# Both parts of the values side by side in a hybrid decoder trunk: 512-column products for a pair of heads, upper keys split too, the block branch stacked

## Chip, cores and metric

The kernel runs on one core of a Trainium2 chip. The metric is the device time of one execution in microseconds (us); less is better. Engines are named as in the profile: PE is the matrix engine (PEld its weight loads), DVE the vector engine, ACT the scalar engine, POOL the GpSimd engine, SP the queue that issues the transfers.

## What is computed

The reference is a two-layer decoder trunk on 256 positions of width 2048, all in float32:

```python
for i in range(DEPTH):                       # DEPTH = 2
    h = rms_norm(x, norm_mix[i])
    x = x + (nsa_mixer(h, ...) if i % 2 == 0 else pool_mixer(h, ...))
    h = rms_norm(x, norm_ffn[i])
    x = x + swiglu(h, ffn_w_gu[i], ffn_w_down[i])
return rms_norm(x, norm_final)
```

The change lies in `nsa_mixer` of layer 0. It has 32 query heads in 4 groups that share keys and values; a key has 96 columns, a value 64. Each head has three attention branches: over 15 compressed blocks (the block branch), over selected blocks, and over a sliding window. At 256 positions selection and window both come out as causal attention over all positions, each with its own keys and values. Each branch is a masked softmax of scores plus a bias by distance, times the values; the three results are weighted by sigmoid gates and added, and the result of all heads is multiplied by `w_out`.

## The kernel before

**Numbers in two parts.** A float32 weight is loaded as `wraw`, copied by ACT into a high part `whi` (L134) in the type fp32r, and DVE subtracts that to give the low part `wlo` (L135). Activations are held in two parts in the same way, next to each other: `xg[k]` is 128 x 512, 256 columns of high part and then 256 of low part. A product is high x high, high x low and low x high. `gemm` (L170) does it as three matmuls of 256 columns for each of 16 steps of k (lines 166 to 168) into one 256-column sum. `gemm2` (L190) sends the high weights once over all 512 columns (L186) and the low weights over 256 (L185, L188), so two sums lie side by side in the bank; `whole` (L216) then adds them: ACT copies one half out (L219), DVE adds the other (L220).

**The stages.** First norm, key and value projections and block compression; then the attention loop over the heads; then the output projection `w_o`, and the feed-forward and pooling stages, all of which stream their weights through PE. The weights come in blocks of 128 x 1024 in one fixed order (`stream`); five blocks are loaded ahead and three are split ahead.

**The attention loop** runs over 8 quads of heads. A quad's queries need three products over `xg` (each 16 steps of k), split into parts by L642 (ACT) and L643 (DVE). Then it goes over two pairs of heads:

- `scores` (L521), for each head: nine matmuls into `ps_s` (three buffers), DVE adds scale and bias on the way out (L540) into `prob` (128 x 768: upper and lower half of the positions, two branches) and into `pc` for the block branch; maxima on DVE (L551, L553), exponentials with their sums on ACT (L557), reciprocals and gates on DVE (L559, L560), scaling on ACT (L563) and DVE (L565).
- `block_scores` (L569), for each pair: one maximum on DVE (L574), four exponentials on ACT (L577), a reciprocal (L579), gate, scale and mask on POOL (L580 to L585).
- `turned` (L588), for each head: four PE transposes (L592) of the probabilities of keys 0 to 127 into `ps_t` (two buffers), a high part by ACT (L595) and a low part by DVE (L596), each 128 x 512.
- `turned_rest` (L599), for each pair: four transposes (L603) of the probabilities of keys 128 to 255 (only the upper 128 positions have any), copied by ACT as plain float32 (L605); two transposes of the block probabilities (L608), copied by DVE (L611, 64 x 256).
- `outputs` (L614), for each head: six matmuls of 256 columns (L620 to L622) with the values `v0h`, `v0l` as weights. The values stand with 64 columns of zeros on each side, and the 128-column slice is taken so that an even head lands in the upper and an odd head in the lower half of the partitions of one sum `ps_o` (one buffer, 128 x 256).
- `outputs_rest` (L624): for each pair four matmuls of 128 columns with plain float32 values (L630; each appears as two instructions in the profile) and one of 256 columns for the block branch (L632, also two).
- ACT and DVE then split `ps_o` into `oT` (L654, L655).

**What sets the order.** The order of each engine's instructions is fixed when the program is built: a planner walks the program with its own model of durations and gives each engine, in turn, the earliest-written instruction that is ready by that model. On the chip every engine works through its list in order. So the query products of the next quad, and near the end the first columns of the output projection (`own=j == 0`, L750), are woven between the steps of a pair. The bias of a head is loaded four heads ahead (L514, L535).

Of the kernel before, what the change touches and what calls it, by code (L numbers as in the profile page):

```python
# [17 lines left out]
P = 128  # L18
# [24 lines left out]
VPAD = (2 * G + 1) * DV  # L43
# [19 lines left out]
def nsa_pool_trunk(ctx, tc, xT, xn, gain0, small, band, gfin, w_kc, w_qk, w_vg, w1k, w1v, w_o,  # L63
# [217 lines left out]
    v0 = {a: ap.tile([P, 2, VPAD], F32R, name=f"v0{a}") for a in "hl"}  # L281
    v1 = ap.tile([P, 2, VPAD], F32, name="v1")
    vc = ap.tile([2 * CB, G, P], F32, name="vc")
# [3 lines left out]
    pcs = [ap.tile([P, 2, 2, CB], F32, name=f"pc{i}") for i in range(3)]  # L287

    def values(t):

        return t[:, DV:].rearrange("p (g z d) -> p g z d", g=G, z=2)[:, :, 0, :]
# [3 lines left out]
    with tc.tile_pool(name="first", bufs=1, reuse_waits="tile") as fp, \  # L295
# [45 lines left out]
        for t in (v0["h"], v0["l"], v1, vc):  # L341
            nc.gpsimd.memset(t.bitcast(F32) if t.dtype == F32R else t, 0.0)
        for t in pcs:
            nc.gpsimd.memset(t, 0.0)
# [107 lines left out]
        def block_values():  # L452
            hv = yield from hidden(vab, "b1v", "v")
            pv = bank()[:NC, :G * DV]
            w2 = col("w2v").rearrange("p (h d) -> p h d", h=2)
            for g in range(G):
                for h in range(2):
                    nc.tensor.matmul(pv[:, g * DV:(g + 1) * DV], hv[:, h, g * CS:g * CS + NC],
                                     w2[:, h], start=h == 0, stop=h == 1)
            for i in range(2):  # L460
                nc.scalar.activation(vc[i * CB:i * CB + NC, :, i * DV:(i + 1) * DV],
                                     pv.rearrange("n (g d) -> n g d", g=G), AF.Copy)


        def row_values(br):
# [15 lines left out]
            h0, l0 = (values(v0[a][:, br]) for a in "hl")  # L481
            nc.scalar.activation(h0, src[0], AF.Copy, scale=rcol[:, 0:1])
            for g in range(G):
                nc.vector.scalar_tensor_tensor(l0[:, g], src[0][:, g], rcol[:, 0:1],
                                               h0[:, g].bitcast(F32), op0=OP.mult, op1=OP.subtract)
            nc.scalar.activation(values(v1[:, br]), src[1], AF.Copy, scale=rcol[:, 1:2])
# [25 lines left out]
    def load_bias(h):  # L512

        bias[h] = hp.tile([P, 400], F32, name="bias", bufs=4)  # L514
        nc.sync.dma_start(bias[h], bass.AP(tensor=skew.tensor, offset=skew.offset + h * 528,
                                           ap=[[1, P], [1, 400]]))
# [4 lines left out]
    def scores(h, qs, pc):  # L521
# [12 lines left out]
        if h + 4 < NH:  # L534
            load_bias(h + 4)  # L535
# [9 lines left out]
        logits(pc[:, 1, e, :CS], ps[0][:, :CS], 1, CB - 1, [[-CS, CS]])  # L545
        logits(view(p, P, [[S, 2], [1, P]]), ps[1], 1, P, two)
        logits(p[:, 512:], ps[2][:, CS:], 0, P, two)
        logits(pc[:, 0, e, :CS], ps[2][:, :CS], 0, P + CB - 1, [[-CS, CS]])
# [20 lines left out]
    def block_scores(h, pc):  # L569

        x = pc[:, :, :, :CS]
        mx = hp.tile([P, 2, 2], F32, name="mxc")
        su = hp.tile([P, 2, 2], F32, name="suc")
        nc.vector.tensor_reduce(mx, x, axis=AX.X, op=OP.max, negate=True)  # L574
        for t in range(2):
            for e in range(2):
                nc.scalar.activation(x[:, t, e], x[:, t, e], AF.Exp, bias=mx[:, t, e:e + 1],  # L577
                                     accum_out=su[:, t, e:e + 1])
# [3 lines left out]
        for t in range(2):  # L582
            nc.gpsimd.tensor_tensor(x[:, t], x[:, t], su[:, t, :, None].to_broadcast([P, 2, CS]),
                                    op=OP.mult)
            nc.gpsimd.tensor_tensor(x[:, t], x[:, t], m[:, t, None, :].to_broadcast([P, 2, CS]),  # L585
                                    op=OP.mult)

    def turned(p):  # L588

        ps = psA.tile([P, 512], F32, name="ps_t", bufs=2)  # L590
        for i, o in enumerate((512, 0, 640, S)):
            nc.tensor.transpose(ps[:, i * P:(i + 1) * P], p[:, o:o + P], ident)  # L592
        th = hp.tile([P, 512], F32R, name="th", bufs=3)
        tl = hp.tile([P, 512], F32R, name="tl", bufs=3)
        nc.scalar.activation(th, ps, AF.Copy)  # L595
        nc.vector.tensor_tensor(tl, ps, th.bitcast(F32), op=OP.subtract)  # L596
        return th, tl

    def turned_rest(p2, pc):  # L599

        ps = psA.tile([P, 512], F32, name="ps_t", bufs=2)
        for i, (p, o) in enumerate(((p2[0], P), (p2[0], S + P), (p2[1], P), (p2[1], S + P))):
            nc.tensor.transpose(ps[:, i * P:(i + 1) * P], p[:, o:o + P], ident)  # L603
        t1 = hp.tile([P, 512], F32, name="t1", bufs=2)
        nc.scalar.activation(t1, ps, AF.Copy)  # L605
        ps = psA.tile([P, 512], F32, name="ps_t", bufs=2)
        for t in range(2):
            nc.tensor.transpose(ps[:2 * CB, t * P:(t + 1) * P],  # L608
                                pc[:, t].rearrange("p e n -> p (e n)"), ident)
        tcm = hp.tile([2 * CB, S], F32, name="tcm", bufs=2)  # L610
        nc.vector.tensor_copy(tcm, ps[:2 * CB, :S])  # L611
        return t1, tcm

    def outputs(h, po, th, tl):  # L614
        g, odd = h // HG, h % 2
        c = DV * (2 * g + 1 - odd)
        for br in range(2):
            va, vb = (v0[a][:, br, c:c + P] for a in "hl")
            xa, xb = th[:, br * S:(br + 1) * S], tl[:, br * S:(br + 1) * S]
            nc.tensor.matmul(po, va, xa, start=not odd and br == 0, stop=False)  # L620
            nc.tensor.matmul(po, va, xb, start=False, stop=False)
            nc.tensor.matmul(po, vb, xa, start=False, stop=False)  # L622

    def outputs_rest(h, po, t1, tcm):  # L624
        g = h // HG
        for e in range(2):
            c = DV * (2 * g + 1 - e)
            for br in range(2):
                i = 2 * e + br
                nc.tensor.matmul(po[:, P:], v1[:, br, c:c + P], t1[:, i * P:(i + 1) * P],  # L630
                                 start=False, stop=False)
        nc.tensor.matmul(po, vc[:, g, :], tcm, start=False, stop=True)  # L632

    for h in range(4):
        load_bias(h)
    for q in range(NH // 4):
# [3 lines left out]
        for j in range(3):  # L640
            ps = whole(gemm2(xg), "up")
# [3 lines left out]
        for h in range(4 * q, 4 * q + 4, 2):  # L645
            pc = pcs[h // 2 % 3]
            p2 = [scores(i, q4 if i % 4 == 3 else q3[:DK, i % 4], pc) for i in (h, h + 1)]
            block_scores(h, pc)
            po = psA.tile([P, 512], F32, name="ps_o")[:, :S]
            for e in range(2):  # L650
                outputs(h + e, po, *turned(p2[e]))
            outputs_rest(h, po, *turned_rest(p2, pc))
            o = oT[h // 2]
            nc.scalar.activation(o[:, :S], po, AF.Copy)  # L654
            nc.vector.tensor_tensor(o[:, S:], po, o[:, :S].bitcast(F32), op=OP.subtract)  # L655
# [293 lines left out]
```

## Time and profile before

| | us |
|---|---|
| median of 3 runs | 2148.22 |
| lowest and highest | 2146.88, 2149.23 |
| the profiled execution | 2149.3 |
| its span, first to last instruction | 2146.6 |
| PE busy / weight loads busy | 2122.3 / 1788.1 |
| DVE busy / ACT busy / POOL busy | 1190.1 / 1055.4 / 62.7 |

In a group's line the numbers behind the bar are the busy time of the whole group in us and the mean duration of one in ns; in a timeline a line begins with the start and the duration in us. A matmul's duration is much longer than the distance to the next one, because they are pipelined: what a matmul costs PE is the distance from its start to the next start. The same holds, by less, for DVE and ACT.

### The profile page before, as it was taken

The numbers are of one execution on the slowest core, as the hardware profiler recorded it, in microseconds if no ns is written. First come the engines' busy times: TensorE is split into PE (matmuls) and PEld (weight loads), VectorE is DVE, ScalarE is ACT, GpSimd is POOL, SyncE is SP. The second block draws the span as 40 slices with busy tenths as digits, with TensorE's granted clock in tenths as the row PEclk, the third lists the DMA queues.
The fourth block names the chain that finished last, engine by engine and source line by source line (L and its number), as shares of the span: only waits on it lengthen the run. The fifth ranks groups of instructions, "written<-read, shape, count | busy, mean of one in ns | idle before, by whom it ended". The sixth has DMA issues, their size and how long they took to land.

```text
span 2146.6 us, 27425 instructions
## 1 busy us (share of the span) xinstructions
PE 2122.3 (99%) x10412; PEld 1788.1 (83%) x10412; DVE 1190.1 (55%) x1534; ACT 1055.4 (49%) x1602; POOL 62.7 (3%) x138
## 2 busy tenths in 40 slices
PE   8999999999999999999999999999999999999997
PEld 7899888888888888888888888888888888888886
DVE  7768888555455445554444555555444554444443
ACT  5578787454444444444344454544444444434443
POOL 4000011000000000000000000000000000000000
PEclk9999999999999999999999999999999999999999
DMA  6674444666666666666666656666666666676664
GB/s 234 193 225 137 143 138 119 193 182 192 189 190 187 192 188 194 188 187 195 188 192 190 196 174 185 184 189 186 190 190 190 192 184 191 189 212 192 193 194 127
DMA packets 115267, 396.78 MB, mean 185 GB/s; under 512 B 13088, under 2 KB 19488, under 8 KB 114880
## 3 DMA queue, kind: packets, MB, share of 16 engines
q1 hardware_dynamic: 115088, 394.97, 61.1%
q8 instruction: 81, 1.33, 0.3%
q14 instruction: 50, 0.41, 0.1%
q10 hardware_dynamic: 48, 0.07, 0.0%
HBM read 391.25 MB, written 2.16 MB: 183 GB/s over the span
## 4 chain that ended last, share of the span: by engine, by line
PE 98%; POOL 1%; DVE 0%; ACT 0%; DMA 0%; issue 0%; SPq 0%; DVEq 0%; POOLq 0%; ACTq 0%
PE acc L212 26%; PE acc L211 26%; PE acc L213 26%; PE acc L186 5%; PE acc L185 2%; PE turn L737 1%; PE ps_t L592 1%; PE acc L166 1%; PE ps_o L630 1%; PE acc L168 1%; PE acc L167 1%; POOL kab L388 1%; PE ps_s L529 1%; PE ps_s L531 1%; PE ps_s L530 1%; PE turn L703 0%
## 5 line engine op out<-in xcount | busy, mean ns | idle before, releaser
L135 DVE TENSOR_TENSOR wlo<-wraw,whi 128x1024 fp32r<-128x1024 f32 (+1 forms) x727 | 886.8, 1221 | 847.0 <-ACT whi L134 840.8
L134 ACT ACTIVATE whi<-wraw 128x1024 fp32r<-128x1024 f32 (+1 forms) x727 | 765.6, 1053 | 912.4 <-PE acc L213 851.3
L213 PE MATMUL acc<-whi,xg 128*128 128x512 f32 x1536 | 599.8, 390 | 0.0
L212 PE MATMUL acc<-wlo,xg 128*128 128x512 f32 x1536 | 598.3, 390 | 0.0
L211 PE MATMUL acc<-whi,xg 128*128 128x512 f32 x1536 | 545.8, 390 | 0.0
L212 PEld LDWEIGHTS acc<-wlo,xg 128*128 128x128 f32 x1536 | 288.4, 188 | 59.3
L213 PEld LDWEIGHTS acc<-whi,xg 128*128 128x128 f32 x1536 | 288.3, 188 | 59.3
L211 PEld LDWEIGHTS acc<-whi,xg 128*128 128x128 f32 x1536 | 288.4, 188 | 58.5
L212 PE MATMUL acc<-wlo,hid 128*128 128x512 f32 x704 | 274.2, 390 | 0.0
L213 PE MATMUL acc<-whi,hid 128*128 128x512 f32 x704 | 274.1, 389 | 0.0
L211 PE MATMUL acc<-whi,hid 128*128 128x512 f32 x704 | 247.4, 390 | 0.0
L186 PE MATMUL acc<-xg,whi 128*128 128x512 f32 x512 | 184.6, 401 | 0.0
L212 PEld LDWEIGHTS acc<-wlo,hid 128*128 128x128 f32 x704 | 132.2, 188 | 27.4
L211 PEld LDWEIGHTS acc<-whi,hid 128*128 128x128 f32 x704 | 132.1, 188 | 27.4
L213 PEld LDWEIGHTS acc<-whi,hid 128*128 128x128 f32 x704 | 132.1, 188 | 27.1
L185 PE MATMUL acc<-xg,wlo 128*128 128x256 f32 x480 | 136.1, 284 | 2.8 <-DVE wlo L135 2.8
L186 PEld LDWEIGHTS acc<-xg,whi 128*128 128x128 f32 x512 | 95.6, 189 | 17.9 <-issue 0.4
L185 PEld LDWEIGHTS acc<-xg,wlo 128*128 128x128 f32 x480 | 91.3, 190 | 4.8 <-DVE wlo L135 3.1
L557 ACT ACTIVATE prob<-prob,mx 128x128 f32<-128x128 f32 (+1 forms) x128 | 56.6, 446 | 5.1 <-DVE mx L551 3.3
L212 PE MATMUL acc<-wlo,oT 128*128 128x512 f32 x128 | 51.1, 399 | 0.0
L213 PE MATMUL acc<-whi,oT 128*128 128x512 f32 x128 | 50.4, 396 | 0.0
L212 PE MATMUL acc<-wlo,mixed 128*128 128x512 f32 x128 | 50.1, 392 | 0.0
(208 smaller groups left out, 1774.5 us busy)
## 6 DMA issues: line engine op xcount, KB each, us to landing
wraw<-in_gu SPq DMA_DIRECT2D x352, 512.0 KB, 3.7
wraw<-in_down SPq DMA_DIRECT2D x176, 512.0 KB, 3.7
wraw<-in_w_qk SPq DMA_DIRECT2D x64, 512.0 KB, 4.1
wraw<-in_w_o SPq DMA_DIRECT2D x32, 512.0 KB, 3.7
wraw<-in_p_in SPq DMA_DIRECT2D x32, 512.0 KB, 3.6
wraw<-in_p_out SPq DMA_DIRECT2D x32, 512.0 KB, 3.6
bias<-skew SPq DMA_DIRECT2D x32, 200.0 KB, 3.5
wraw<-in_p_grp SPq DMA_DIRECT2D x8, 512.0 KB, 3.7
```

Source lines behind the costliest of these rows:

```text
L134: nc.scalar.activation(hi[:, :n], t[:, :n], AF.Copy)
L135: nc.vector.tensor_tensor(lo[:, :n], t[:, :n], hi[:, :n].bitcast(F32), op=OP.subtract)
L166: nc.tensor.matmul(ps, hi, x[:, :S], start=first, stop=False)
L167: nc.tensor.matmul(ps, hi, x[:, S:], start=False, stop=False)
L168: nc.tensor.matmul(ps, lo, x[:, :S], start=False, stop=last)
L185: nc.tensor.matmul(*lows, start=False, stop=False)
L186: nc.tensor.matmul(ps, hi, x, start=first, stop=last)
L211: nc.tensor.matmul(ps[t], xa, hi, start=k == 0, stop=False)
L212: nc.tensor.matmul(ps[t], xa, lo, start=False, stop=False)
L213: nc.tensor.matmul(ps[t], xb, hi, start=False, stop=k == n - 1)
L388: nc.gpsimd.tensor_tensor(t[DK:, :, j, g, :], src[r, g, :, 3, :], w[r, :, 3, None].to_broadcast([32, KQ, CS]), op=OP.add)
L557: nc.scalar.activation(p[:, o:o + n], p[:, o:o + n], AF.Exp, bias=mx[:, i:i + 1], accum_out=su[:, i:i + 1])
```

## The change

- **Values side by side.** `v0h`, `v0l`, `v1` and their zero columns go. `vv[t]` holds, for each half t of the keys, each branch and group, 64 columns of high part followed by 64 of low part; row_values makes both parts for both halves. As weights they give, in one matmul, the high-part result in partitions 0 to 63 and the low-part result in 64 to 127.
- **A pair streams as 512 columns.** `turned` takes four pieces of both heads for one branch. For each branch, the high and the low part of the probabilities go through `vv[0]` as one matmul of 512 columns each. The upper keys are turned and split in the same way and go through `vv[1]` in four matmuls of 256 columns, in place of plain float32.
- **Blocks stacked.** The block values stand as high, low, high part in 48 rows (`vc`, put there by three transfers), and the block probabilities as high, high, low part, so that one fp32r matmul of 512 columns does the branch. `block_scores` moves the shift of the maximum, the scaling and the low part to POOL, takes one exponential and one double copy on ACT and sums on DVE.
- **Joining the halves.** After the last product DVE copies partitions 64 to 127 of the sum out (`low`) and adds them to partitions 0 to 63; then ACT and DVE split the two heads separately.
- **Queries by `gemm`.** The three query products of a quad use `gemm` in place of `whole(gemm2(...))`.
- Buffers: the bias is loaded three heads ahead (3 buffers, 4 before), `th` and `tl` have 4 (3 before); the `pc` tiles are no longer cleared on POOL.

```diff
+            for t in range(2):
+                h, l = (vv[t][:, br, :, i * DV:(i + 1) * DV] for i in range(2))
+                nc.scalar.activation(h, src[t], AF.Copy, scale=rcol[:, t:t + 1])
+                for g in range(G):
+                    nc.vector.scalar_tensor_tensor(l[:, g], src[t][:, g], rcol[:, t:t + 1],
...
-        for t in range(2):
-            for e in range(2):
-                nc.scalar.activation(x[:, t, e], x[:, t, e], AF.Exp, bias=mx[:, t, e:e + 1],
-                                     accum_out=su[:, t, e:e + 1])
+        nc.gpsimd.tensor_tensor(pc, pc, spread4(mx), op=OP.add)
+        nc.scalar.activation(pc, pc, AF.Exp)
+        nc.vector.tensor_reduce(su, pc, axis=AX.X, op=OP.add)
         nc.vector.reciprocal(su, su)
         nc.gpsimd.tensor_tensor(su, su, gatec[:, :, h:h + 2], op=OP.mult)
+        nc.gpsimd.tensor_tensor(pc, pc, spread4(su), op=OP.mult)
...
+        nc.gpsimd.tensor_tensor(pc, pc, m[:, :, None, :].to_broadcast([P, 2, 2, CS]), op=OP.mult)
+        nc.scalar.activation(y[:, :, :2], x[:, :, None, :].to_broadcast([P, 4, 2, CS]), AF.Copy)
+        nc.gpsimd.tensor_tensor(y[:, :, 2], x, y[:, :, 0].bitcast(F32), op=OP.subtract)
...
+    def turned_blocks(pc):
+                nc.tensor.transpose(ps[:3 * CS, i * P:(i + 1) * P],
+        tcm = hp.tile([3 * CS, 512], F32R, name="tcm", bufs=1)
+        nc.vector.tensor_copy(tcm, ps[:3 * CS])
...
+    def outputs(h, p2, pc):
+        po = psA.tile([P, 512], F32, name="ps_o")
+        for br in range(2):
+            first = turned([p[:, o:o + P] for p in p2 for o in (512 + br * P, br * S)])
+            for i, x in enumerate(first):
+                nc.tensor.matmul(po, vv[0][:, br, g], x, start=br == 0 and i == 0, stop=False)
+        last = turned([p[:, br * S + P:(br + 1) * S] for br in range(2) for p in p2])
+        for x in last:
+            for br in range(2):
+                nc.tensor.matmul(upper, vv[1][:, br, g],
+                                 x[:, br * S:(br + 1) * S].rearrange("p (e s) -> p e s", e=2),
+                                 start=False, stop=False)
+        nc.tensor.matmul(po, vc[:, g], turned_blocks(pc), start=False, stop=True)
+        low = hp.tile([DV, 512], F32, name="low", bufs=1)
+        nc.vector.tensor_copy(low, po[DV:])
+        nc.vector.tensor_tensor(po[:DV], po[:DV], low, op=OP.add)
+        o = oT[h // 2]
+        for e in range(2):
+            src, dst = po[:DV, e * S:(e + 1) * S], o[e * DV:(e + 1) * DV]
+            nc.scalar.activation(dst[:, :S], src, AF.Copy)
+            nc.vector.tensor_tensor(dst[:, S:], src, dst[:, :S].bitcast(F32), op=OP.subtract)
...
-            ps = whole(gemm2(xg), "up")
+            ps = gemm(xg)
```

More of the change, by code (lines that the diff above doesn't have):

```diff
@@ L42 @@
 QT = NH // 4 * 3
-VPAD = (2 * G + 1) * DV
 KQ = CS // 4
@@ L339, in nsa_pool_trunk @@
         nc.vector.tensor_scalar(rq, rcol, DK ** -0.5, None, op0=OP.mult)
[L341 to L344, printed above, removed]
+        nc.gpsimd.memset(vc.bitcast(F32), 0.0)
         for a in "hl":
@@ L459, in block_values @@
                                      w2[:, h], start=h == 0, stop=h == 1)
[L460 to L462 removed]
+            src = pv.rearrange("n (g d) -> n g d", g=G)
+            part = [fp.tile([NC, G, DV], F32R, name=f"vp{i}") for i in range(2)]
+            nc.scalar.activation(part[0], src, AF.Copy)
+            nc.vector.tensor_tensor(part[1], src, part[0].bitcast(F32), op=OP.subtract)
+            for i, x in enumerate((0, 1, 0)):
+                nc.sync.dma_start(vc[i * CS:i * CS + NC, :, :DV].bitcast(F32),
+                                  part[x].bitcast(F32))
         def row_values(br):
@@ L480, in row_values @@
             src = [p[:, :G * DV].rearrange("s (g d) -> s g d", g=G) for p in ps]
[L481 to L486, printed above, removed]
+            for t in range(2):
[3 more added lines that the diff above has]
+                    nc.vector.scalar_tensor_tensor(l[:, g], src[t][:, g], rcol[:, t:t + 1],
+                                                   h[:, g].bitcast(F32), op0=OP.mult,
+                                                   op1=OP.subtract)
             for t in range(2):
@@ L590, in turned @@
+        x = pc.rearrange("p t e n -> p (t e) n")
+        y = parts.rearrange("p t e i n -> p (t e) i n")
+        nc.scalar.activation(y[:, :, :2], x[:, :, None, :].to_broadcast([P, 4, 2, CS]), AF.Copy)
+        nc.gpsimd.tensor_tensor(y[:, :, 2], x, y[:, :, 0].bitcast(F32), op=OP.subtract)
+        return parts
+    def turned(pieces):
         ps = psA.tile([P, 512], F32, name="ps_t", bufs=2)
-        for i, o in enumerate((512, 0, 640, S)):
-            nc.tensor.transpose(ps[:, i * P:(i + 1) * P], p[:, o:o + P], ident)
@@ L593, in turned @@
-        th = hp.tile([P, 512], F32R, name="th", bufs=3)
-        tl = hp.tile([P, 512], F32R, name="tl", bufs=3)
+        for i, x in enumerate(pieces):
+            nc.tensor.transpose(ps[:, i * P:(i + 1) * P], x, ident)
+        th = hp.tile([P, 512], F32R, name="th", bufs=4)
+        tl = hp.tile([P, 512], F32R, name="tl", bufs=4)
         nc.scalar.activation(th, ps, AF.Copy)
@@ L614, in outputs @@
-    def outputs(h, po, th, tl):
-        g, odd = h // HG, h % 2
-        c = DV * (2 * g + 1 - odd)
-        for br in range(2):
[L618 to L625, printed above, removed]
-        for e in range(2):
[L627 to L632, printed above, removed]
@@ L635, in nsa_pool_trunk @@
+    for h in range(3):
         load_bias(h)
@@ L645, in nsa_pool_trunk @@
         for h in range(4 * q, 4 * q + 4, 2):
-            pc = pcs[h // 2 % 3]
+            pc = hp.tile([P, 2, 2, CS], F32, name="pc", bufs=3)
             p2 = [scores(i, q4 if i % 4 == 3 else q3[:DK, i % 4], pc) for i in (h, h + 1)]
[L648 to L655, printed above, removed]
+            pc = block_scores(h, pc)
+            outputs(h, p2, pc)
     at.close()
```

49 lines of the change are left out of this document (17 added, 32 removed).

## The prediction

> **What bounds the kernel now.** I read the page first: the busy times and the chain that ended last.
>
> ```profile
> PE 2122.3 (99%) x10412; PEld 1788.1 (83%) x10412; DVE 1190.1 (55%) x1534; ACT 1055.4 (49%) x1602; POOL 62.7 (3%) x138
> PE 98%; POOL 1%; DVE 0%; ACT 0%; DMA 0%; issue 0%; SPq 0%; DVEq 0%; POOLq 0%; ACTq 0%
> ```
>
> PE sets the time nearly everywhere, so whatever shortens PE's list should shorten the kernel, as long as nothing else comes up to it. But 55% of DVE is a mean over stages. The change touches the attention loop, so I asked for the busy times there: from 142 us, where the loop's work on DVE begins, to 372, where that of the last pair thins out; the tail up to 391; and two dense stretches.
>
> ```profile
> core 0: us, PE busy (x) PEld busy (x) DVE busy (x) ACT busy (x) POOL busy (x), PEclk, DMA share, GB/s
> 142.00:372.00 230.00, 230.00 (x1523) 205.76 (x1522) 198.80 (x526) 186.74 (x582) 21.82 (x75) 1.00 0.45 138
> 372.00:391.00 19.00, 18.53 (x107) 15.38 (x106) 9.74 (x17) 10.20 (x27) 2.10 (x5) 1.00 0.53 163
> 150.00:164.00 14.00, 14.00 (x92) 12.61 (x91) 13.85 (x44) 14.00 (x48) 2.34 (x5) 1.00 0.59 173
> 170.00:180.00 10.00, 10.00 (x71) 8.90 (x70) 9.98 (x25) 7.44 (x25) 0.00 (x0) 1.00 0.46 149
> ```
>
> PE never rests in the loop, but DVE is at 198.80 of 230 us (86%) and in places at 99%. In the 249 us of both windows DVE has 31.2 + 9.3 = 40.5 us of idle time. That is the room for anything the change gives to DVE; it is the number on which the rest turns.
>
> **PE: what a pair of heads costs, before and after.** The distance from start to start is the price. Three places of PE's timeline:
>
> ```profile
> 347.47 0.39 PE L186 MATMUL acc<-xg,whi 128*128 128x512 f32 x1
> 347.70 0.28 PE L185 MATMUL acc<-xg,wlo 128*128 128x256 f32 x1
> 347.82 1.05 PE L630 MATMUL ps_o<-t,v 128*128 128x128 f32 x8
> 348.71 0.60 PE L592 MATMUL ps_t<-ident,prob 128*128 128x128 f32 x4
> 349.06 0.47 PE L186 MATMUL acc<-xg,whi 128*128 128x512 f32 x1
> ...
> 365.03 0.40 PE L211 MATMUL acc<-whi,oT 128*128 128x512 f32 x1
> 365.35 0.70 PE L632 MATMUL ps_o<-tcm,vc 64*128 64x256 f32 x2
> 365.98 0.50 PE L212 MATMUL acc<-wlo,oT 128*128 128x512 f32 x1
> 366.32 0.39 PE L213 MATMUL acc<-whi,oT 128*128 128x512 f32 x1
> ...
> 373.66 0.28 PE L620 MATMUL ps_o<-th,v0h 128*128 128x256 f32 x1
> 373.77 0.28 PE L621 MATMUL ps_o<-tl,v0h 128*128 128x256 f32 x1
> 373.89 0.28 PE L622 MATMUL ps_o<-th,v0l 128*128 128x256 f32 x1
> ```
>
> So 512 columns of fp32r take 0.23, 256 take 0.117, four turns take 0.35 (0.0875 each), a pair's eight upper-key instructions take 0.89. The block product sits in a stretch of 365.03 to 366.32, 1.29, with two 512-column matmuls; less 2 x 0.23 it costs 0.83. Two halves of 256 cost the same as one 512, so the width itself saves nothing. What saves is that the zero columns go, and that plain float32 becomes fp32r.
>
> Before, a pair: 12 x 0.117 = 1.40 for L620 to L622, 0.89, 0.83, and 14 turns, 1.23: together 4.35. After: four of 512 and four of 256 for the values, 0.92 + 0.47, one of 512 for the blocks, 0.23, and 16 turns, 1.40: together 3.02. The difference is 1.33 a pair, over 16 pairs 21.3 us. The stacked block product has 48 rows, a form the trace lacks; its price lies between 0.23 (the fp32r rows) and 0.83 (the only short one, 64 rows of float32). I take 0.23, since all fp32r rows keep to the column count; the other end would cost 9.6 us of PE. A step of the query products is 0.23 + 0.12 = 0.35 before and 3 x 0.117 = 0.35 after: nothing. Three loads of weights in place of two are hidden there, as they are in the L620 rows, where every matmul brings its own. If PE stayed the bound, the kernel would be 21 us shorter.
>
> **DVE: what is added.** A run of DVE's timeline without idle time, and three groups from the groups by shape in 142 to 391:
>
> ```profile
> 218.08 0.21 DVE L574 TENSOR_REDUCE mxc<-pc 128x4 f32<-128x64 f32 x1
> 218.21 0.15 DVE L560 TENSOR_TENSOR su<-su,gates 128x4 f32<-128x4 f32 x1
> 218.28 0.68 DVE L596 TENSOR_TENSOR tl<-ps_t,th 128x512 fp32r<-128x512 f32 x1
> 218.88 0.41 DVE L655 TENSOR_TENSOR oT<-ps_o,oT 128x256 fp32r<-128x256 f32 x1
> 219.21 0.47 DVE L565 TENSOR_SCALAR prob<-prob,su 128x128 f32<-128x128 f32 x2
> ```
>
> ```profile
> L220 DVE TENSOR_TENSOR up<-acc,up 128x256 f32<-128x256 f32 x22 | 9.1, 416 | 1.4 <-ACT up L219 1.4
> L655 DVE TENSOR_TENSOR oT<-ps_o,oT 128x256 fp32r<-128x256 f32 x16 | 6.7, 416 | 4.2 <-ACT oT L654 4.2
> L611 DVE COPY tcm<-ps_t 64x256 f32<-64x256 f32 x16 | 6.6, 412 | 4.3 <-PE ps_t L608 4.0
> ```
>
> From start to start 512 elements cost 0.60, 256 cost 0.33 and the small reduction 0.13; L220 and L611 last as long as L655, so 0.33 too, on 64 partitions as on 128. Per pair come: the low part of the upper keys 0.60; `tcm` of 512 in place of 256, 0.27; `low` 0.60; the join 0.60; a second split of `oT` 0.33; the block sum 0.13. What goes is 1.5 x L220, 0.50. The sum is +2.03 a pair, 32.5 us over 16 pairs. The join reads and writes PSUM, which no row in the loop does. I bound it by 0.33 (the 256-element row) and 1.20 (a read and a write pass in turn), and take 0.60, the row of its length; the ends shift the total by -4 and +10 us.
>
> **ACT and POOL.** Four exponentials of the block branch with their sums, and what follows them:
>
> ```profile
> 373.56 0.30 ACT L577 ACTIVATE pc<-pc,mxc 128x16 f32<-128x16 f32 x1
> ...
> 374.72 1.06 ACT L134 ACTIVATE whi<-wraw 128x1024 fp32r<-128x1024 f32 x1
> ```
>
> These 1.16 us a pair become one exponential and one copy, each short (0.3 at most by the row's duration); 1.5 copies of `whole` go too and one `oT` copy comes. ACT is eased by at least half a us a pair. It was at 186.74 of 230 and does not bind. POOL gets wider steps, but at 21.82 of 230 it can double and stay idle most of the time; the block branch is needed last in a pair, so a longer chain there lies beside the other products.
>
> Three transfers for `vc` go onto SP's list ahead of weight loads and wait for a small ACT and a DVE step; five loads ahead cover that, and without the cover it is one wait of a few us. The bias one head less ahead still has two heads' time. Clearing less on POOL happens in the first 6 us, away from any waiting: nothing. The four extra DVE steps in each row_values, some 2 us together, fall where PE is the bound.
>
> **The sum.** PE's list ends 21.3 us earlier, DVE's grows by 32.5 into 40.5 us of room. With DVE never idle the loop could end 40.5 - 32.5 = 8.0 us earlier, not 21.3: DVE takes over as the bound. And DVE can't be without idle time. In the dense stretches it rests 0.15 of 14 and 0.02 of 10 us, so I leave 1.5% of 230, 3.5 us, for the loop. In the tail it follows one pair through PE and ACT and rests 9.3 of 19; part of that was PE busy with products that would have run earlier under a DVE bound, so I leave 5. That uses 8.5 of the 8.0: +0.5 us, no change. On the profiled execution's 2149.3 (a span of 2146.6 and 2.7 around it) that is 2149.8; the median of the runs shown is 1.1 lower, so the forecast is 2148.7. A measurement of this kernel can tell about 0.2%, 4.3 us, from no change. Idle leftovers between 5 and 16 us give 2145 to 2156 for this case; the join's bounds stretch that to 2141 and, half-way to its far end, 2160.
>
> What DVE waits for now is mostly not of its own making; the two longest lines of its waits in 142 to 372:
>
> ```profile
> DVE prob L540 <- PE ps_s L531: 8.6, 14, 1.4
> DVE wlo L135 <- ACT whi L134: 7.1, 13, 1.3
> ```
>
> Both come from engines that will have more time ahead of DVE. That speaks for small leftovers. The largest single wait is 1.4 us. Where PE waits long, its clock shows it:
>
> ```profile
> 40.00:60.00 20.00, 15.53 (x86) 12.99 (x85) 14.30 (x19) 9.21 (x13) 16.63 (x26) 0.98 0.40 130
> 60.00:80.00 20.00, 20.00 (x109) 17.34 (x108) 15.40 (x23) 8.73 (x12) 0.00 (x0) 0.94 0.63 184
> ```
>
> After 4.5 us of rest in 20 the next 20 us were granted 0.94, a loss of 1.2 us. PE's new idle time should come in pieces as small as DVE's waits, so I charge nothing. The Trainium skill, "TensorE: Matmul & The Clock Gate", Part 1, says that one idle window of about 3.4 us halves the clock until a busy one has passed; by it each such gap would add some 1.7 us (3.4 at half speed, an estimate from that page), a rule against this change, which gives PE its first idle time in the loop.
>
> **Rivals.** *Faster: DVE keeps up.* If the new DVE steps come nearer to their low bounds and the leftovers to 4 us, the loop ends 4 to 14 us earlier; the limit is PE's 21.3, 2127. For it: 99% in the dense stretches with PE at 100%. Against it: PE and DVE would both have to be nearly full for 230 us. Middle value 2138.
>
> *Slower: the one `ps_o` bank.* Its place is between two pairs. The bank was free again after one ACT and one DVE step; now a copy of 0.60, a join of 0.60, and the two halves' splits follow each other, with DVE's other work in between. PE works in order: if the next pair's first value product stands in its list before the bank is free, the query products and scores behind it wait, and DVE then lacks its inputs. For it: DVE will be full, so each of these steps queues behind others, a `wlo` of 1.1 us for instance. Against it: between L632 (365.35) and the next pair's L620 (373.66) there are 8.3 us. It decides once the join is late by more than that slack; at 0.5 us a pair it costs 8 us, 2156, at 1 us 16 us, 2164.
>
> *Slower: POOL and DVE in each other's way.* The same two POOL steps, beside a `wlo` and alone:
>
> ```profile
> 156.81 1.53 POOL L585 TENSOR_TENSOR pc<-pc,sm 128x32 f32<-128x32 f32 x2
> ...
> 166.96 0.47 POOL L585 TENSOR_TENSOR pc<-pc,sm 128x32 f32<-128x32 f32 x2
> 157.02 1.21 DVE L135 TENSOR_TENSOR wlo<-wraw,whi 128x1024 fp32r<-128x1024 f32 x1
> ```
>
> POOL took 1.06 us longer when `wlo` started within its step. If the blocking also goes the other way, wider POOL steps hold up the three `wlo` of a pair; at 0.25 us each that is 12 us, 2160. It decides only with DVE as the bound. The Trainium skill, "SBUF — State Buffer", Who interferes with whom, says that a DVE instruction with two SBUF inputs and a GpSimd one that reads SBUF exclude each other for a whole instruction; the first pair of rows agrees, DVE being held has no row here.
>
> **Chances.** Forecast 0.41; DVE keeps up 0.30; the bank 0.21; POOL 0.08. So faster 0.30, same 0.41, slower 0.29. The likeliest time is 2148.7, its own range 2141 to 2160. For 8 in 10 the range goes from 2135 (most of the faster case) to 2162 (the bank at 0.85 us a pair, POOL in full).
>
> **What would show it.** In the profile after: PE's instructions for a pair cost 3.0 us; DVE's busy share of the loop rises from 86% to 97% or more; PE, without a wait in the loop now, shows idle time ended by DVE (`tl`, `wlo`, `oT`), some 20 us in all. The chain that ended last passes through DVE in the loop. I am wrong if PE still has no idle time there (then -21), if DVE's idle time stays above 16 us (the bank, or order), or if `low` and the join last much longer than 0.68.

## The result, and the profile after

The changed kernel takes 2170.6 us (median of four runs, 2168.81 to 2170.91) against 2148.31 in the same session: a ratio of 1.0104, 95% interval 1.0092 to 1.0116. It is 1% slower, 21.9 us above the forecast and outside its range. The profiled execution has a span of 2168.8 us, 22.2 more than before.

The page's busy times and its chain that ended last, after the change:

```profile
PE 2124.3 (98%) x10620; PEld 1798.7 (83%) x10620; DVE 1222.5 (56%) x1599; ACT 1042.2 (48%) x1497; POOL 74.6 (3%) x132
PE 95%; DVE 3%; POOL 1%; ACT 0%; DMA 0%; issue 0%; SPq 0%; DVEq 0%; POOLq 0%; ACTq 0%
```

DVE now holds 3% of the chain, where it held none, and PE 95 in place of 98. To see what that is in the loop I cut the loop at the one event that both kernels have: the start of the block product of the last pair (before, the second of its two instructions of L632; after, L630). First the row of before from 142 us to that event, then the two of after, up to 372 and from there on.

```profile
142.00:389.30 247.30, 247.30 (x1624) 220.46 (x1623) 208.11 (x541) 196.56 (x606) 23.92 (x80) 1.00 0.45 138
```

```profile
core 0: us, PE busy (x) PEld busy (x) DVE busy (x) ACT busy (x) POOL busy (x), PEclk, DMA share, GB/s
142.00:372.00 230.00, 222.71 (x1665) 208.75 (x1665) 211.23 (x528) 164.37 (x444) 36.36 (x70) 0.98 0.49 147
372.00:407.65 35.65, 24.36 (x115) 18.45 (x113) 26.84 (x69) 19.60 (x60) 2.87 (x10) 0.86 0.16 53
```

The third busy time of a row is DVE's. Before, DVE worked 208.1 us up to the event and rested 39.2. After, it worked 211.23 + 26.84 = 238.1 and rested 18.8 + 8.8 = 27.6. So the event comes 30.0 - 11.6 = 18.4 us later by this sum (407.65 against 389.3 by the clock). Another 3.8 us come behind it: 22.2 in all. There PE waits for the last pair's `oT`: the next L210 starts 3.3 us after the event (before, L211 0.85 us after it), and the clock granted from 410.7 to 414.2 us is 0.51. PE, which had no idle time up to this event, has 7.3 + 11.3 = 18.6 us of it.

DVE's groups by shape in the loop show that the added steps have the sizes forecast:

```profile
L632 DVE COPY low<-ps_o 64x512 f32<-64x512 f32 x16 | 11.1, 693 | 7.4 <-PE ps_o L630 7.0
L633 DVE TENSOR_TENSOR ps_o<-ps_o,low 64x512 f32<-64x512 f32 x16 | 10.9, 683 | 0.1
L609 DVE CAST tcm<-ps_t 48x512 fp32r<-48x512 f32 x16 | 10.8, 673 | 0.4 <-PE ps_t L606 0.3
```

The join (L633) reads and writes PSUM and still lasts 683 ns, like every other step of 512 elements. The waits of PE and of DVE, the first from 142 to 412, the second from 142 to 372 (what is waited for: total, times, longest):

```profile
PE acc L210 <- ACT oT L637: 6.0, 3, 3.3
PE ps_t L594 <- DVE tl L598: 5.6, 4, 2.8
PE ps_t L594 <- DVE prob L562: 4.7, 2, 2.3
PE ps_t L594 <- DVE tcm L609: 2.2, 2, 1.4
```

```profile
DVE wlo L134 <- ACT whi L133: 5.1, 8, 1.4
DVE prob L537 <- PE ps_t L594: 4.0, 4, 2.2
DVE low L632 <- PE ps_o L630: 2.8, 4, 1.1
DVE su L556 <- ACT prob L554: 2.4, 2, 1.4
```

PE waits for DVE's results, DVE in between for ACT's and PE's. All of PE's idle time up to the event lies after 312 us, and its clock falls there. Four windows of 20 us:

```profile
340.00:360.00 20.00, 15.80 (x90) 12.66 (x88) 19.88 (x54) 11.92 (x37) 0.58 (x2) 0.90 0.40 113
360.00:380.00 20.00, 17.37 (x85) 13.44 (x85) 17.15 (x51) 13.76 (x44) 2.66 (x10) 0.84 0.10 33
380.00:400.00 20.00, 13.38 (x62) 9.84 (x62) 15.46 (x42) 11.66 (x36) 2.58 (x9) 0.83 0.08 27
400.00:420.00 20.00, 14.52 (x52) 10.96 (x50) 8.61 (x14) 5.92 (x12) 0.00 (x0) 0.83 0.43 157
```

Why so late shows in the order. Counted in the trace at 300 us, before had scored 22 heads and done 18.8 of the 24 query products of the loop; after, 20 heads and 21.6 products. While DVE lags, PE works on the next quads' query products, which stand early in its list. They are used up at about 325 us (some 350 before), and then PE has nothing to put between the steps of a pair.

The hand-off of the last pair but one, on DVE's timeline and on PE's:

```profile
399.63 0.69 DVE L632 COPY low<-ps_o 64x512 f32<-64x512 f32 x1
400.36 0.68 DVE L609 CAST tcm<-ps_t 48x512 fp32r<-48x512 f32 x1
400.96 0.68 DVE L633 TENSOR_TENSOR ps_o<-ps_o,low 64x512 f32<-64x512 f32 x1
401.56 1.21 DVE L134 TENSOR_TENSOR wlo<-wraw,whi 128x1024 fp32r<-128x1024 f32 x1
402.69 0.41 DVE L638 TENSOR_TENSOR oT<-ps_o,oT 64x256 fp32r<-64x256 f32 x1
403.55 0.42 DVE L638 TENSOR_TENSOR oT<-ps_o,oT 64x256 fp32r<-64x256 f32 x1 [0.44 <-ACT oT L637]
```

```profile
398.68 0.49 PE L630 MATMUL ps_o<-tcm,vc 48*128 48x512 f32 x1
399.10 0.73 PE L212 MATMUL acc<-whi,oT 128*128 128x512 f32 x2
399.67 0.60 PE L606 MATMUL ps_t<-ident,pcp 128*48 128x128 f32 x4
403.57 0.52 PE L210 MATMUL acc<-whi,oT 128*128 128x512 f32 x1 [3.30 <-ACT oT L637]
...
405.16 0.63 PE L622 MATMUL ps_o<-th,vv 128*128 128x512 f32 x1
```

From the block product (398.68) to the first use of this pair's `oT` (403.57) go 4.9 us of steps in a row. PE stands 3.3 us before a matmul of the output projection (L210), and the next pair's value products (L622) stand behind it in PE's list although their inputs are there.

### The profile page after: what moved, and what is told of

It is laid out like the page before. It is cut to its first block, busy times and chain, and to the rows that moved or that the text cites. A ratio compares the mean times of both kernels' runs of the same rounds, so it can differ in the third digit from the quotient of the medians.

```text
span 2168.8 us, 27851 instructions
## 1 busy us (share of the span) xinstructions
PE 2124.3 (98%) x10620; PEld 1798.7 (83%) x10620; DVE 1222.5 (56%) x1599; ACT 1042.2 (48%) x1497; POOL 74.6 (3%) x132
## 4 chain that ended last, share of the span: by engine, by line
PE 95%; DVE 3%; POOL 1%; ACT 0%; DMA 0%; issue 0%; SPq 0%; DVEq 0%; POOLq 0%; ACTq 0%
PE acc L210 26%; PE acc L211 26%; PE acc L212 26%; PE acc L165 3%; PE acc L167 3%; PE acc L166 3%; PE turn L737 1%; PE ps_t L594 1%; PE acc L185 1%; PE ps_o L622 1%; POOL kab L380 1%; PE turn L703 0%; PE ps_s L526 0%; DVE wlo L134 0%; PE ps_s L527 0%; PE ps_s L528 0%
## 5 line engine op out<-in xcount | busy, mean ns | idle before, releaser
L211 PE MATMUL acc<-wlo,xg 128*128 128x512 f32 x1536 | 598.3, 390 | 0.0
L210 PE MATMUL acc<-whi,xg 128*128 128x512 f32 x1536 | 545.9, 390 | 0.0
L211 PEld LDWEIGHTS acc<-wlo,xg 128*128 128x128 f32 x1536 | 288.4, 188 | 59.2
L210 PEld LDWEIGHTS acc<-whi,xg 128*128 128x128 f32 x1536 | 288.5, 188 | 58.6
L211 PE MATMUL acc<-wlo,hid 128*128 128x512 f32 x704 | 274.2, 390 | 0.0
L210 PE MATMUL acc<-whi,hid 128*128 128x512 f32 x704 | 247.4, 390 | 0.0
L211 PEld LDWEIGHTS acc<-wlo,hid 128*128 128x128 f32 x704 | 132.2, 188 | 27.4
L210 PEld LDWEIGHTS acc<-whi,hid 128*128 128x128 f32 x704 | 132.2, 188 | 27.1
L165 PE MATMUL acc<-xg,whi 128*128 128x256 f32 x432 | 124.3, 289 | 5.3 <-ACT whi L133 5.3
L166 PE MATMUL acc<-xg,whi 128*128 128x256 f32 x432 | 124.0, 289 | 0.0
L167 PE MATMUL acc<-xg,wlo 128*128 128x256 f32 x432 | 121.0, 287 | 0.6 <-DVE wlo L134 0.6
L165 PEld LDWEIGHTS acc<-xg,whi 128*128 128x128 f32 x432 | 83.5, 193 | 6.4 <-ACT whi L133 5.9
L166 PEld LDWEIGHTS acc<-xg,whi 128*128 128x128 f32 x432 | 83.6, 194 | 0.2
L167 PEld LDWEIGHTS acc<-xg,wlo 128*128 128x128 f32 x432 | 81.9, 193 | 1.3 <-DVE wlo L134 0.8
L210 PE MATMUL acc<-whi,oT 128*128 128x512 f32 x128 | 51.0, 420 | 6.1 <-ACT oT L637 6.0
```

Of the source, the lines that this page charges most:

```text
L165: nc.tensor.matmul(ps, hi, x[:, :S], start=first, stop=False)
L166: nc.tensor.matmul(ps, hi, x[:, S:], start=False, stop=False)
L167: nc.tensor.matmul(ps, lo, x[:, :S], start=False, stop=last)
L210: nc.tensor.matmul(ps[t], xa, hi, start=k == 0, stop=False)
L211: nc.tensor.matmul(ps[t], xa, lo, start=False, stop=False)
```

## The experiments

The theory to test: with the new steps DVE is the bound, but an ordered list with hand-offs between three engines can't fill it as far as the forecast had it, and what DVE lags by comes out at the end of the loop, where PE has no other work. Rivals: the single `ps_o` bank; the query products running ahead; the new query form; POOL in DVE's way; the length of the hand-off by itself. The kernels on one table, cut at the start of the last block product as above (DVE's work and idle time from 142 us to it); an "idle step" is one whose result nobody uses. The median is that of all runs of a kernel; the last three columns are those of its one profiled execution, which lies up to 2.8 us from the median (with the two copies on ACT 2159.16, with less run-ahead 2164.85):

| kernel | median us | ratio to before (95%) | DVE busy | DVE idle | event at |
|---|---|---|---|---|---|
| before | 2148.31 | | 208.1 | 39.2 | 389.3 |
| after | 2170.6 | 1.0104 (1.0092 to 1.0116) | 238.1 | 27.6 | 407.7 |
| before, one idle step a head | 2147.71 | 1.0000 (0.9990 to 1.0009) | 223.1 | 23.5 | 388.6 |
| before, two idle steps a head | 2158.36 | 1.0051 (1.0036 to 1.0066) | 240.0 | 17.6 | 399.6 |
| before, queries by `gemm` | 2151.03 | 1.0015 (1.0006 to 1.0024) | 199.8 | 49.8 | 391.6 |
| before, low parts on POOL | 2149.4 | 1.0008 (0.9999 to 1.0018) | 176.4 | 70.7 | 389.1 |
| after, no join | 2148.07 | 1.0000 (0.9991 to 1.0009) | 220.0 | 25.6 | 387.6 |
| after, two copies on ACT | 2156.41 | 1.0041 (1.0026 to 1.0056) | 218.5 | 34.7 | 395.2 |
| after, less run-ahead | 2167.21 | 1.0088 (1.0073 to 1.0103) | 236.1 | 23.1 | 401.2 |
| after, two `ps_o` and two `ps_s` banks | 2165.91 | 1.0085 (1.0068 to 1.0101) | 239.7 | 19.2 | 400.9 |
| after, one `ps_o` and two `ps_s` banks | 2168.14 | 1.0097 (1.0082 to 1.0112) | 238.1 | 23.5 | 403.6 |
| after, low parts on POOL | 2148.66 | 1.0006 (0.9996 to 1.0015) | 207.6 | 34.9 | 384.5 |
| after, join off DVE | 2145.72 | 0.9988 (0.9978 to 0.9997) | 214.4 | 29.9 | 386.3 |
| the same, wide queries | 2154.23 | 1.0035 (1.0022 to 1.0049) | 226.7 | 23.0 | 391.7 |

**Load alone, on the kernel before.** In `turned`, one or two maxima of 512 elements for each head:

```diff
+        junk = hp.tile([P, 2], F32, name="junk")
+        for i in range(2):                    # range(1) in the other kernel
+            nc.vector.tensor_reduce(junk[:, i:i + 1], th.bitcast(F32), axis=AX.X, op=OP.max)
```

> Kernel before with idle work for DVE: after each head's low part one maximum over the 128x512 high part, 0.60 us, whose result nobody reads; 1.2 us a pair, 19 us in all, nothing else changed. It asks how much of DVE's 40 us of room can be used while PE's list stays as it was. Theory D in the form of the forecast (all but some 8 us of the room can be filled): within 3 us of before. If the room is mostly not to be had, because DVE waits in order for PE and ACT: 8 to 19 us slower.

> The same with two such maxima after each head's low part: 2.4 us a pair, 38 us in all, a little over the change's 32. Theory D as in the forecast: 40 us of room less 38, with 8 us that cannot be used, 4 to 10 us slower than before. If the room is mostly not to be had: 20 to 38 us slower.

One step a head changes nothing (2147.71), two cost 10.6 us by the medians of that session (2158.36 against 2147.79), a little over the 4 to 10 expected. The row of the one-step kernel, from the groups by shape, has 676 ns each, as for the other steps of 512 elements; at their 0.60 us from start to start, 32 of them are 19 us of work and 64 are 38:

```profile
L599 DVE TENSOR_REDUCE junk<-th 128x1 f32<-128x512 f32 x32 | 21.6, 676 | 0.0
```

So the form of the forecast holds: DVE's idle time takes up load for nothing, until it is gone. But it is gone earlier than forecast. The busy times with two steps, from 142 to 372 and on to the event:

```profile
142.00:372.00 230.00, 226.60 (x1465) 200.70 (x1464) 213.87 (x538) 176.64 (x538) 21.80 (x70) 1.00 0.48 145
372.00:399.60 27.60, 26.00 (x159) 21.93 (x158) 26.10 (x68) 19.65 (x70) 3.21 (x10) 0.90 0.24 85
```

In a loop of the old form with DVE as the bound, 16.1 us of the first 230 and 1.5 of the last 27.6 stay idle. This kernel's query products run ahead as well (20 heads and 20.6 products at 300 us).

**The join taken out.** After, without `low` and the join, so that the products with the values' low parts don't reach the output:

```diff
-        low = hp.tile([DV, 512], F32, name="low", bufs=1)
-        nc.vector.tensor_copy(low, po[DV:])
-        nc.vector.tensor_tensor(po[:DV], po[:DV], low, op=OP.add)
```

> Changed kernel without the copy of the low half and the join: the products with the low parts of the values are left out of the result. DVE loses 1.2 us a pair, 19 us in all, as in the run that moved two copies to ACT (2156); but here the chain from the last product of a pair to the free bank also gets 1.2 us shorter, while there it kept its length. Theory D: the same DVE time, so the same result, 2152 to 2160. Theory B: the shorter hand-off counts too, 2135 to 2150.

2148.07: the whole loss goes, 22.5 us, with 18 us of DVE's busy time. The load alone was expected to give 2152 to 2160; the time lies in the range of the rival that counts the shorter hand-off too.

**The same relief with the chain as long.** After, the two copies `low` and `tcm` on ACT:

```diff
-        nc.vector.tensor_copy(tcm, ps[:3 * CS])
+        nc.scalar.activation(tcm, ps[:3 * CS], AF.Copy)
...
-        nc.vector.tensor_copy(low, po[DV:])
+        nc.scalar.activation(low, po[DV:], AF.Copy)
```

> Changed kernel with the two copies out of PSUM (the turned block probabilities and the low half of the sum) on ACT in place of DVE. DVE loses 1.2 us a pair, 19 us in all; ACT, at 69% of the loop, takes about as much. Theory D (DVE is the bound, its added steps are the cost): 15 to 25 us faster than the changed kernel, so 2146 to 2156. Theory O (the order of PE's list: query products run ahead early, so that late in the loop PE has nothing to fill with): 5 to 12 us faster, since DVE's list is shorter in the late part only; 2159 to 2166. Theory B (the one bank of the sum): the hand-off keeps its length, within 4 us of 2171.

2156.41, just outside the 2146 to 2156 expected from the load. DVE's busy time up to the event is the same as without the join (218.5 and 220.0), yet the kernel is 8.3 us slower. The waits of PE tell where:

```profile
PE acc L210 <- ACT oT L637: 4.3, 2, 2.7
PE ps_t L594 <- ACT tcm L609: 3.6, 2, 3.3
```

So DVE's load isn't all of it. The likely reason is that steps which stand one behind the other between two pairs cost as well, on whichever engine they are. But ACT does 201 us of work up to the event here against 183, so these 8 us are not shown to be the hand-off's alone.

**The bank.** `ps_s` with two buffers and `ps_o` with two (so that the two hold as many banks together as without the edit), and as a control `ps_s` with two alone:

```diff
-            o = psA.tile([P, 512], F32, name="ps_s", bufs=3)[:, :n]
+            o = psA.tile([P, 512], F32, name="ps_s", bufs=2)[:, :n]
...
-        po = psA.tile([P, 512], F32, name="ps_o")
+        po = psA.tile([P, 512], F32, name="ps_o", bufs=2)
```

> Changed kernel with two banks for the sum of a pair, and two in place of three for the scores. Theory B: the join no longer holds up the next pair; 8 to 20 us faster than the changed kernel, 2151 to 2163. Theory D and O: no gain from the bank, and the scores have one bank less; within 4 us of 2171 or up to 10 us slower.

> Changed kernel with two in place of three banks for the scores and still one bank for the sum of a pair: the counterpart of the run with two banks for the sum, which took 2166. Theory D: the second bank of the sum does nothing, so this one also takes 2163 to 2169. Theory B: the bank gained about 10 us there and the missing scores bank took some of it back; 2172 to 2182 here.

2165.91 against 2168.14 in the control (ratio 1.0097, 1.0082 to 1.0112): the intervals overlap, and at most a few of the 22 us are the bank's, not the 8 to 20 that this rival was expected to show. PE's waits after the change name no `ps_o` bank that DVE or ACT had yet to free.

**The running ahead.** After, with one buffer for `q3` and `q4` (`bufs=1` added to each):

> Changed kernel with one buffer in place of two for a quad's queries, so that the query products can run less far ahead of the heads. Theory O: PE's fill is left for the late part of the loop, its idle time there shrinks and its clock stays up; 8 to 18 us faster than the changed kernel, 2153 to 2163. Theory D: DVE's work is the same and it now also waits for queries at the start of each quad; within 4 us of 2171 or slower, up to 2185. Theory B: within 4 us.

2167.21, within the 4 us of 2171 that the load theory gave it; the order alone was expected to bring 8 to 18. At 300 us there are 22 heads scored and 20.0 products done, so PE's order is most of the way back to that of before, and 3.4 of the 22 us come back. The running ahead says where the idle time falls; for most of it, it isn't the cause.

**The query form.** The kernel before, with queries by `gemm` alone:

```diff
-            ps = whole(gemm2(xg), "up")
+            ps = gemm(xg)
```

> Kernel before with one part of the change alone: the query products as three matmuls of 256 columns without the joining of two halves. PE pays 0.01 us more for each of 384 steps (0.36 against 0.35), 4 us; DVE loses 0.33 us and ACT 0.27 us for each of 24 products, 8 and 6 us. Theory D and O: the kernel before is bound by PE, so 2 to 5 us slower than before, 2150 to 2153. If DVE had held the kernel before back somewhere it would be faster, 2142 to 2147.

2151.03 against 2147.59 in its session, ratio 1.0015: DVE lost 8 us of work, and the kernel became 3.4 us slower. The forecast had this at nothing for PE. PE's timeline after the change shows the price:

```profile
195.83 0.28 PE L167 MATMUL acc<-xg,wlo 128*128 128x256 f32 x1
195.95 0.28 PE L165 MATMUL acc<-xg,whi 128*128 128x256 f32 x1
196.07 0.28 PE L166 MATMUL acc<-xg,whi 128*128 128x256 f32 x1
196.19 0.28 PE L167 MATMUL acc<-xg,wlo 128*128 128x256 f32 x1
```

A matmul of 256 columns comes every 0.12 us here, not 0.117: 0.36 a step in place of 0.35, and 384 steps make 3.8 us.

**Low parts on POOL.** The `wlo` of 48 blocks of query weights in pieces of 256 columns on POOL, in the kernel after and in the one before:

```diff
+        if b in queries:
+            for o in range(0, n, 256):
+                c = slice(o, o + 256)
+                nc.gpsimd.tensor_tensor(lo[:, c], t[:, c], hi[:, c].bitcast(F32), op=OP.subtract)
+        else:
+            nc.vector.tensor_tensor(lo[:, :n], t[:, :n], hi[:, :n].bitcast(F32), op=OP.subtract)
```

> Changed kernel with the low parts of the query weights (48 blocks of 128x1024, 1.13 us each on DVE, 54 us in all) on POOL, in pieces of 256 columns. DVE then has less to do in the loop than before the change. Theory D: PE is the bound again and shows what the change saves there, 21 us by the forecast less 4 for the dearer query steps and 3 for the block product: 2130 to 2140. Theory O (order alone): the planner still runs query products ahead where it can; 2150 to 2165. If POOL and DVE hold each other up: above 2160.

> Kernel before with the low parts of the query weights on POOL in the same way, nothing else. PE is its bound, so with 54 us taken off DVE the time should not move: within 4 us of before. If POOL is too slow for the stream (about 0.7 us for 256 columns by the rows of the block stage) or holds DVE up, it is slower by 5 us or more.

2148.66 and 2149.4 (ratio 1.0008, 0.9999 to 1.0018). With DVE's load taken off, the change costs nothing; in the kernel before the same relief is worth nothing, since PE is the bound there. The 2130 to 2140 expected of the first failed, by what PE's list turns out to cost (below). DVE's relief is smaller than the blocks moved: up to the event DVE makes 10 `wlo` in place of 50, some 49 us, and its busy time falls by 30.5. A part of the difference is that POOL now holds DVE up: the scaling L568 (L562 without the edit) from the groups by shape, with the edit and without:

```profile
L568 DVE TENSOR_SCALAR prob<-prob,su 128x128 f32<-128x128 f32 x64 | 25.7, 440 | 0.2
```

```profile
L562 DVE TENSOR_SCALAR prob<-prob,su 128x128 f32<-128x128 f32 x64 | 15.5, 280 | 0.1
```

**The join off DVE, the bank free early.** After, but ACT copies both halves out of `ps_o` (`top`, `low`), POOL joins them in SBUF and makes the low parts:

```diff
-        nc.vector.tensor_copy(low, po[DV:])
-        nc.vector.tensor_tensor(po[:DV], po[:DV], low, op=OP.add)
+        nc.scalar.activation(top, po[:DV], AF.Copy)
+        nc.scalar.activation(low, po[DV:], AF.Copy)
+        nc.gpsimd.tensor_tensor(top, top, low, op=OP.add)
+        nc.scalar.activation(high, top, AF.Copy)
...
-            nc.scalar.activation(dst[:, :S], src, AF.Copy)
-            nc.vector.tensor_tensor(dst[:, S:], src, dst[:, :S].bitcast(F32), op=OP.subtract)
+            nc.scalar.activation(dst[:, :S], high[:, c].bitcast(F32), AF.Copy)
+            nc.gpsimd.tensor_tensor(dst[:, S:], top[:, c], high[:, c].bitcast(F32), op=OP.subtract)
```

> Changed kernel with the bank of the sum emptied by two ACT copies at once; the join and the low parts of the result are made on POOL from SBUF, the high parts on ACT. DVE loses the copy, the join and both splits, 1.87 us a pair, 30 us in all, and is about where it was before the change; the bank is free after 1.2 us; ACT gets some 1.8 us a pair more. Theory D and B both: PE becomes the bound, 2132 to 2146, faster than the kernel before. Theory O (order alone): 2148 to 2160.

2145.72, ratio 0.9988 (0.9978 to 0.9997): the fastest of all, though the gain over before is at the edge of what can be told. Last, this kernel with the wide query products back:

> The kernel with the short hand-off (two ACT copies empty the bank, the join and the low parts on POOL) measured 2145.72, with PE's waits left only in 369 to 393 us and DVE at 214 of 249 us. Here its query products go back to the wide form with its two halves added afterwards. By the rows, PE saves some 4 us (48 query sums of 16 steps at 0.12 less per three matmuls measured in the changed kernel against 0.117 in the form before, and steps of 0.35 against 0.36), DVE gets 24 adds of 0.33, 8 us, back, ACT 24 copies of 0.4, 10 us. Theory that a nearly full DVE lets the query products run ahead and leaves the late loop bare: DVE would be at 222 of 249, as full as with one idle step per head, which was free; so PE's saving shows, 2141 to 2144. Rival that the length of the hand-off between pairs alone counted: the same, since the chain is unchanged; but ACT, now on that chain with four copies and at 210 of 249, goes to 220, and if its queue sets the end the time is above 2148. No change from 2145.7 (within 1.5 us) would say that the query form is of no weight in either kernel.

2154.23. The expected 2141 to 2144 failed by more than 10 us; the rival's sign came true. The rows up to the event, without and with the wide form, and PE's longest waits with it:

```profile
142.00:386.30 244.30, 240.15 (x1792) 223.18 (x1791) 214.40 (x537) 207.31 (x548) 81.13 (x125) 0.99 0.50 152
```

```profile
142.00:391.70 249.70, 239.59 (x1442) 204.76 (x1440) 226.68 (x557) 214.75 (x569) 87.40 (x125) 0.99 0.45 137
```

```profile
PE ps_o L622 <- ACT th L597: 3.7, 2, 2.2
PE ps_o L622 <- DVE tl L598: 2.1, 4, 1.1
```

12 us more on DVE and 7 on ACT made the loop 5 us longer, although neither is above 91% of it, and the products ran ahead again (20 heads, 21.7 products at 300 us; 23 and 19.8 without). "As full as with one idle step per head, which was free" doesn't carry over: the old form could take 223.1 us of DVE work, this one not 226.7 beside a busier ACT. Which of the two engines it is wasn't separated.

## Why the prediction was wrong

**DVE's list: right.** 32.5 us were forecast; measured are 30.0 in busy time up to the event, which leaves out the last pair's join. The join took the middle value.

**DVE becomes the bound: right.** PE rests in the loop for the first time, mostly behind DVE, and taking DVE's steps away (no join, low parts on POOL) removes the loss, while the same relief in the kernel before brings nothing.

**The idle time that DVE keeps: the step that failed.** "In the dense stretches it rests 0.15 of 14 and 0.02 of 10 us, so I leave 1.5% of 230, 3.5 us, for the loop", and 5 in the tail: 8.5. Measured are 18.8 and 8.8, together 27.6: 19.1 more, of a miss of 21.9. Two short stretches in which DVE happened to have a backlog were taken as the rate of a whole loop. The kernel before with two idle steps shows the rate for nearly the same load (240.0 us) in the old form: 17.6 idle, 16.1 of them in the first 230 us, that is 93% full. So some 9 of the 19 us are what such a load leaves in the old form too. Of the 18.8 us, 12.8 lie before 312 us, where PE has no idle time at all (DVE 157.2 of 170); from 340 to 360, where PE waits, DVE rests 0.12 of 20. So most of what DVE loses up to 372 us it loses while PE has other products to run. Waits for `whi` from ACT and for scores and sums in turn are what the profile names there; that the fixed order of the lists makes them is argued, not shown.

**The other 10 us: the new form of a pair.** With about the same DVE work, two idle steps end the loop 8 us earlier than the change does, though PE has the longer list there. Most of the extra idle time lies in the tail: 8.8 us against 1.5. There stand the long hand-off (copy, join, two splits in turn, a `wlo` of 1.2 us between) and PE behind L210. That its length counts is what the two reliefs of equal size point to, 2148.07 and 2156.41, but ACT's load differs between them. PE's slow clock (below) is in it as well. The share of each stays open.

**"Part of that was PE busy with products that would have run earlier under a DVE bound, so I leave 5."** That was in the forecast, as a reason for a small leftover in the tail. The products did run earlier, and what it brought was the reverse: the late pairs had nothing beside them.

**"PE's new idle time should come in pieces as small as DVE's waits, so I charge nothing."** Wrong too. PE's waits reach 3.3 us, and the clock is 0.83 to 0.90 from 340 to 420. By those four rows 61.1 us of PE's work ran at some 0.85 (estimate from these rows: about 9 us lost), part of it beside other waits. On the page PE is busy 2.0 us longer than before, 2124.3 against 2122.3, although its list is shorter. The same matmul on PE's timeline, at 374 and at 389 us:

```profile
374.66 0.39 PE L622 MATMUL ps_o<-tl,vv 128*128 128x512 f32 x1
374.89 0.39 PE L622 MATMUL ps_o<-th,vv 128*128 128x512 f32 x1
...
381.46 0.41 PE L594 MATMUL ps_t<-ident,prob 128*128 128x128 f32 x2 [2.83 <-DVE tl L598]
383.29 0.59 PE L594 MATMUL ps_t<-ident,prob 128*128 128x128 f32 x2 [1.42 <-DVE tcm L609]
386.21 1.11 PE L594 MATMUL ps_t<-ident,prob 128*128 128x128 f32 x4 [2.34 <-DVE prob L562]
...
388.83 0.63 PE L622 MATMUL ps_o<-th,vv 128*128 128x512 f32 x1
389.26 0.63 PE L622 MATMUL ps_o<-tl,vv 128*128 128x512 f32 x1
```

From start to start 0.23 became 0.43, after three waits of which the longest was 2.83 us; the clock granted from 387 to 390 us was 0.50. The rule that the prediction set against the change (the Trainium skill, "TensorE: Matmul & The Clock Gate", Part 1: an idle window of about 3.4 us halves the clock) had the right effect, but no single wait here was that long. Nor do smaller pieces protect the clock:

```profile
352.70:356.10 3.40, 1.83 (x14) 1.35 (x12) 3.37 (x11) 2.94 (x11) 0.00 (x0) 1.00 0.25 50
356.10:359.50 3.40, 1.76 (x7) 1.03 (x6) 3.40 (x9) 1.28 (x3) 0.00 (x0) 0.51 0.25 64
```

In the first of these stretches PE worked 1.83 of 3.4 us and its longest wait was 1.21 us; in the second it was granted half. So a stretch that was only half idle, in two waits, was followed by the slow clock. What the slow clock costs the kernel wasn't separated from the waits. Of DVE's 8.8 us of rest in the tail, 3.7 lie between 403.96 us and the event, where it waits for the last pair's products and PE runs them at half speed.

**PE's list: some 11 us shorter, not 21.3.** The stacked block product costs more than 0.23. From its start to the next it takes 0.43, but the forecast had measured the old one, 0.83, by the whole stretch with its neighbours. The same here, in a stretch at full clock:

```profile
375.60 0.40 PE L627 MATMUL ps_o<-tl,vv 128*128 128x256 f32 x2
375.92 0.50 PE L630 MATMUL ps_o<-tcm,vc 48*128 48x512 f32 x1
376.35 0.73 PE L212 MATMUL acc<-whi,oT 128*128 128x512 f32 x2
376.92 0.29 PE L526 MATMUL ps_s<-kth,q 96*128 96x272 f32 x1
```

From 375.60 to 376.92 are 1.32 us; less 0.23 for two of 256 columns and 0.46 for two of 512 it costs 0.63, two thirds of the way to the other bound: 0.40 a pair, 6.4 us in all. The query step adds 3.8. Beside a DVE bound this hardly matters, but it is why the kernels with DVE relieved don't reach 2127: 11 us less than before would be 2137, they lie at 2146 to 2149. The rest is mostly PE's waits, 6 to 7 us in the late pairs. With low parts on POOL the page has PE busy for 2113.0 us, 9.3 less than before, and idle for 31.3 of its span of 2144.3, 7.0 more.

**Rivals.** *DVE keeps up* is out: DVE's load ends the loop. *The `ps_o` bank* had the right place, the hand-off between pairs, and the wrong mechanism: a second bank brought 2.2 us against its control, and the intervals of the two overlap. *POOL and DVE*: not in the changed kernel, where `wlo` lasts 1213 ns on the mean and 1222 before; only the edit with low parts on POOL brought it about. The shorter lead of the bias and the three transfers for `vc` weren't tested alone; from 100 to 412 us the profile after the change names no wait of DVE or PE for a transfer. **What would show it** caught the case: "I am wrong if DVE's idle time stays above 16 us (the bank, or order)"; it is 27.6.

## What to carry to other kernels

Before giving work to an engine with x us of idle time, ask how full it gets when it is the bound: here 92 to 93% of 230 us in the loop, not the 99% of its densest stretches; the cheapest way to know is to add idle steps to the kernel at hand until the time moves. A step put between two pairs can be paid twice, as load and as length of the hand-off; here the second showed where the filling work had run out, though its share wasn't measured alone. And when the bound moves to another engine, the order of the old one changes with it: look at what its list has left for the end.

## What the runs showed of the hardware

- A DVE scaling of 128 x 128 from SBUF to SBUF went from 280 to 440 ns on the mean when POOL subtracted weights beside it (the rows above); it is a step with one tile as input and a column of factors. In the trace 28 of the 64 overlap such a POOL step and take 625 ns on the mean, the other 36 take 296. The Trainium skill, "SBUF — State Buffer", Who interferes with whom, counts `tensor_scalar` among the steps that can lock the ports shared with GpSimd; these rows agree, and give the direction that the prediction had no row for.
- A fp32r matmul with 48 rows and 512 columns took 0.43 us to the next start, against 0.23 with 128 rows; in the stretch with its neighbours it cost 0.63.
- PE ran at about half speed (0.43 for 0.23) after waits of 2.83, 1.42 and 2.34 us with a little work between them. Another time the granted clock fell to 0.51 right after 3.4 us in which PE had worked 1.83 us and waited at most 1.21 us at a time.
- A DVE step that reads and writes PSUM lasted about as long (683 ns) as one that reads PSUM and writes SBUF (693 and 673).
